# FFN input products: shared sums carried between PSUM banks, seven products in another order

## Chip, core and metric

The kernel runs as one program on one core of a Trainium2 chip. The metric is the time of one execution in device microseconds (us). TensorE multiplies, VectorE and ScalarE do the elementwise work, GpSimd does next to nothing here, and SyncE issues the DMAs. In the rows PE is TensorE, PEld its weight loads, DVE VectorE, ACT ScalarE, POOL GpSimd, and SPq the DMA queue of SyncE.

## What is computed

One Conformer-style layer over 1056 tokens (1024 of a prompt and 32 of a running stream): a half-step SwiGLU feed-forward block (FFN 1), a mixer of a convolution branch and a recurrent branch, a second feed-forward block (FFN 2), and norms between them. The change lies in the first half of both feed-forward blocks:

```python
D_MODEL = 1024
D_FF = 2816
...
def _swiglu_half_step(x, g_pre, g_post, w_in, w_out):
    h = _rmsnorm(x, g_pre)
    gate, up = jnp.split(h @ w_in, 2, axis=-1)
    return x + 0.5 * _rmsnorm((jax.nn.silu(gate) * up) @ w_out, g_post)
```

## The kernel before

Channels lie on the 128 lanes and tokens along the rows, in four quarters of 264 tokens. All products keep float32's accuracy: each operand is split into a high and a low part, and each term of a product takes three matmuls (`mm3`, L202 wh·xh, L203 wh·xl, L204 wl·xh), each 128x128 by 128x264. Splitting an operand is one copy on ScalarE (L91, the high part) and one subtraction on VectorE (L88, the low part).

An FFN's hidden layer has 22 chunks of 128 channels. The first few (three in FFN 1, two in FFN 2) are plain products. For each of the others, 39 in all, `w_ops` makes seven weight operands w1 to w7 from the gate and up columns of the chunk (Winograd's form of a 2 by 2 cut: rows gate and up, inner halves of the channels, columns two quarters of the tokens). The operands w1, w2 and w4 are split straight from the weights as loaded. The other four come from sums on VectorE in one buffer `s` and one `s3`: w5 from s = a21 + a22, w6 from s - a11 (in place, after w5's parts are read), w7 from s3 = a11 - a21, w3 from a12 - s (in place again). Then `swiglu` runs twice, for the two pairs of quarters (call 0 and call 1 below), 78 calls in all. A call runs seven products of 12 matmuls each, and combines them to silu(gate) * up for two quarters (`prod`), which a DMA stores in DRAM (`hd`, L437). Names in the rows: `p` is a product's PSUM bank, `w` and `xh`/`xl` are operands, `m`, `g`, `u` are sums of products. In the listings of instructions `p6_1_10_0` is product 6 of FFN 1, chunk 10, call 0.

The PSUM pool `ps` has six banks (L63). In each call before, every product gets its own bank: order 1, 2, 4, 5, 6, 7, 3. ScalarE copies product 1 out to `m`, and VectorE forms all sums from `m` and the banks, in nine instructions.

Each engine runs its instructions in the order of its queue, and waits on semaphores. What stands ahead of what in a queue is set by priorities at build time: weight operands are made ready some 100 to 350 instructions early (`WLATE`, `WAHEAD`, `AHEAD`), and everything else comes in the order of the code.

After the hidden chunks the output half of the FFN (bank `po`, operands `hh`, `hl` from loads `hf`, and `wh_o`, `wl_o` from loads `w_o`) multiplies by w_out. SyncE issues the stores `hd`, and the loads `hf` and `w_o`, from one queue.

Of the kernel before, what the change touches and what calls it, by code (L numbers as in the profile page):

```python
# [11 lines left out]
OP = mybir.AluOpType  # L12
# [22 lines left out]
# how many instructions early operands are made ready: weights, those of the seven products, the hidden, w_out's  # L35
AHEAD, WAHEAD, WLATE, HAHEAD, OAHEAD = 350, 120, 100, 100, 150
# terms of products that TensorE runs while a norm's squares, its power, a chain of two norms, a mean, a layer norm
# are on the way, and between the norms of two quarters
SQ, TURN, CHAIN, MUW, LNW, STAG = 12, 6, 30, 16, 32, 32
# chunks of the output that the last two quarters take one after the other; chunks side by side at a pass's start  # L40
TAIL1, TAIL2, TAILW, OG = 4, 3, 2, 2
# hidden chunks by plain products at the start of either FFN
NP = (3, 2)
# taps of the long convolution between the steps of the mixer
# [8 lines left out]
def macaron_kernel(ctx: ExitStack, tc: tile.TileContext, a: dict, o: dict):  # L53
# [43 lines left out]
    def over(x, n):  # L97
        """A [P, w] row seen n times."""
        return bass.AP(tensor=x.tensor, offset=x.offset, ap=[list(x.ap[0]), [0, n], list(x.ap[1])])
# [75 lines left out]
    def load(dst, src):  # L175
        """A load that does not run ahead of the weights traced before it."""
        with tc.issue_after(newest[0]):
            nc.sync.dma_start(dst, src)
# [11 lines left out]
    def after(n, f):  # L190
        """f(), traced when TensorE has n more terms of products to run."""
        later.append((terms[0] + n, f))
# [8 lines left out]
    def mm3(out, wh, wl, xh, xl, first, last):  # L201
        nc.tensor.matmul(out, wh, xh, start=first, stop=False)  # L202
        nc.tensor.matmul(out, wh, xl, start=False, stop=False)  # L203
        newest_mm[:] = [nc.tensor.matmul(out, wl, xh, start=False, stop=last).ins]  # L204
        terms[0] += 1
        for e in [e for e in later if e[0] <= terms[0]]:
            later.remove(e)
            e[1]()
# [33 lines left out]
    def rstd(ssum, name, then, wait=SQ):  # L242
        """then(1 / rms on every lane); TensorE runs other products while the squares are summed and the power is taken."""
# [26 lines left out]
    def pre_norm(x, g, name, then, wait=SQ):  # L270
        """then(half, x / rms * g as a float32 quad), for either half of the channels."""
# [17 lines left out]
    def pre_norm_parts(x, g, name, rb, stored=False):  # L289
        """Parts of x * rb * g; x: quads, or the slice of them that DRAM holds."""  # L290
# [16 lines left out]
    def evacuate(y, c, p, gain, sq, q, name, total=None):  # L307
        """One chunk of the channels of a quarter, times its gain, to y; its squares to the quarter's sum."""
# [11 lines left out]
    def post_norm(y, q, ssum, xsrc, xdst, name, then):  # L320
        """y <- x + y / rms, for one quarter of the tokens, y times its gain already; then()."""
# [16 lines left out]
    #   rows: gate | up; inner: halves of the channels; columns: two quarters of the tokens  # L338
# [8 lines left out]
    def x_part(r, v, half, odd, name):  # L347
        """The parts of half a quarter: two operands each, but for an odd quarter's first half, which only plain products take."""
# [5 lines left out]
    def x_sums(r, fe, fo, name):  # L354
# [12 lines left out]
        tt(t, t, fe[1], OP.subtract)  # L367
# [31 lines left out]
    def swiglu(w, x, prod, name):  # L399
        """prod <- silu(gate) * up of one hidden chunk, two quarters of the tokens."""  # L400
        b = {}

        def product(k):
            b[k] = BANK(f"p{k}_{name}")[:, :N]
            for j in range(HC):
                s = slice(j * P, (j + 1) * P)
                mm3(b[k], w[k][:, 0, s], w[k][:, 1, s], x[k][0][:, j, :], x[k][1][:, j, :], j == 0, j == HC - 1)

        m, g0, g1, u1 = (TMP(f"{n}_{name}") for n in ("m", "g0", "g1", "u1"))
        product("1")  # L410
        copy(m, b["1"])
        product("2")
        tt(g0, m, b["2"], OP.add)
        nc.scalar.activation(g0, g0, AF.Silu)
        product("4")
        product("5")
        product("6")
        tt(m, m, b["6"], OP.add)
        tt(g1, m, b["5"], OP.add)
        product("7")  # L420
        tt(m, m, b["7"], OP.add)
        tt(u1, m, b["5"], OP.add)
        tt(m, m, b["4"], OP.subtract)
        tt(prod[:, 0, :], g0, m, OP.mult)
        product("3")
        tt(g1, g1, b["3"], OP.add)
        nc.scalar.activation(g1, g1, AF.Silu)  # L427
        return tt(prod[:, 1, :], g1, u1, OP.mult).ins

# [1 line left out]
    def ffn(x, f, h, first, mid, w_in, w_out, early, between, finish, tail, n):  # L431
# [41 lines left out]
        for c in range(2):  # L473
# [16 lines left out]
            def out(tiles, blks, which, c=c, hid=hid, y=y):  # L490
                """Tiles (m, q) of the output, together where the hidden chunks are still coming in."""
# [81 lines left out]
    def pieces(q, gap):  # L573
        """The columns of quarter q in a row that keeps `gap` past columns between the two streams."""
# [17 lines left out]
    # the 31 taps by pairs of columns: with E, O the taps at even and odd distances,  # L592
    #   even = E u_even + O u_odd (one pair back), odd = (E + O)(u_even + u_odd) - E u_even - O u_odd
# [346 lines left out]
```

## Time and profile before

| | |
|---|---|
| runs | 2369.85 and 2373.73 us, median 2371.79 us |
| span of the profiled execution | 2369.3 us, first to last instruction; no other time of it is given, and the runs' median lies 2.5 us above it |
| TensorE busy | 2329.1 us (98%) in 19136 matmuls |
| VectorE busy | 1607.6 us (68%) |
| ScalarE busy | 932.3 us (39%) |
| chain that ended last | TensorE 95% |

Matmuls overlap: one is recorded with 0.28 us, while the next starts 0.12 us after it. So a stage is costed by the spacing of the starts, and the busy share shows only where TensorE stood still.

### The profile page before, as it was taken

To read this page: it belongs to the slowest core of one execution; us is meant where nothing else is said; L and a number is where in the kernel's file an instruction comes from. 1 tells how busy PE (TensorE), PEld (TensorE's weight loads), DVE (VectorE), ACT (ScalarE), POOL (GpSimd) and SP (SyncE) were. 2 spreads that over 40 slices of the span, in tenths; PEclk is the share of its full clock that TensorE was granted. 3 is DMA by queue.
4 is the path that set the end of the run, shared out by engine and by line. 5 is a ranking of instruction groups with operands and counts; after the bars stand their busy time and mean duration, and the time that the engine had idled before them with its cause. 6 is when DMAs were issued, how large, how long until landed. Compare 5 with 4: busy or idle time off the path is not lost.

```text
span 2369.3 us, 45071 instructions
## 1 busy us (share of the span) xinstructions
PE 2329.1 (98%) x19136; PEld 2322.5 (98%) x19136; DVE 1607.6 (68%) x2652; ACT 932.3 (39%) x1536; POOL 42.3 (2%) x63
## 2 busy tenths in 40 slices
PE   7999999999999999999999999999999999999996
PEld 7999999999999999999999999999999999999996
DVE  6776666752647887897778966458866666752646
ACT  4333333342444554345544343244333333342432
POOL 0000000000000000000000000001000000000000
PEclk9999999999999999999999999999999999999998
DMA  5122222363655222222222554444122222363453
GB/s 173 60 73 77 82 82 82 106 205 100 230 170 177 74 91 70 85 73 82 75 72 77 179 201 164 146 129 145 59 80 82 82 82 82 96 206 109 168 174 128
DMA packets 126089, 274.13 MB, mean 116 GB/s; under 512 B 16704, under 2 KB 58432, under 8 KB 125888
## 3 DMA queue, kind: packets, MB, share of 16 engines
q1 hardware_dynamic: 125888, 271.26, 35.0%
q8 instruction: 149, 2.44, 0.4%
q14 instruction: 52, 0.43, 0.1%
HBM read 212.55 MB, written 58.67 MB: 114 GB/s over the span
## 4 chain that ended last, share of the span: by engine, by line
PE 95%; DVE 2%; DMA 1%; issue 1%; ACT 0%; POOL 0%; SPq 0%; POOLq 0%; DVEq 0%; ACTq 0%
PE p L202 11%; PE p L204 11%; PE p L203 11%; PE po L203 7%; PE po L202 7%; PE po L204 7%; PE pm L202 3%; PE pm L204 3%; PE pm L203 3%; PE pco L202 1%; PE pco L204 1%; PE pcv L202 1%; PE pcg L202 1%; PE pro L202 1%; PE pco L203 1%; PE prx L202 1%
## 5 line engine op out<-in xcount | busy, mean ns | idle before, releaser
L202 PE MATMUL p<-xh,w 128*128 128x264 f32 x2184 | 620.9, 284 | 1.1 <-ACT w L91 0.8
L203 PE MATMUL p<-xl,w 128*128 128x264 f32 x2184 | 618.7, 283 | 0.1
L204 PE MATMUL p<-xh,w 128*128 128x264 f32 x2184 | 618.5, 283 | 0.0
L202 PEld LDWEIGHTS p<-xh,w 128*128 128x128 f32 x2184 | 410.1, 188 | 2.4 <-ACT w L91 2.4
L203 PEld LDWEIGHTS p<-xl,w 128*128 128x128 f32 x2184 | 411.1, 188 | 0.3 <-DVE xl L88 0.3
L204 PEld LDWEIGHTS p<-xh,w 128*128 128x128 f32 x2184 | 410.0, 188 | 0.0
L203 PE MATMUL po<-hl,wh_o 128*128 128x264 f32 x1408 | 399.4, 286 | 1.8 <-DVE hl L88 1.8
L204 PE MATMUL po<-hh,wl_o 128*128 128x264 f32 x1408 | 398.2, 285 | 0.0
L202 PE MATMUL po<-hh,wh_o 128*128 128x264 f32 x1408 | 393.1, 287 | 1.9 <-ACT hh L91 1.9
L203 PEld LDWEIGHTS po<-hl,wh_o 128*128 128x128 f32 x1408 | 266.2, 189 | 2.6 <-DVE hl L88 2.5
L204 PEld LDWEIGHTS po<-hh,wl_o 128*128 128x128 f32 x1408 | 266.1, 189 | 0.0
L202 PEld LDWEIGHTS po<-hh,wh_o 128*128 128x128 f32 x1408 | 262.1, 189 | 2.7 <-ACT hh L91 2.5
L88 DVE TENSOR_TENSOR wl_o<-w_o,wh_o 128x1024 fp32r<-128x1024 f32 x109 | 132.9, 1224 | 115.3 <-ACT wh_o L91 115.0
L88 DVE TENSOR_TENSOR m<-m,p 128x264 f32<-128x264 f32 x234 | 99.8, 426 | 162.7 <-PE p L204 161.0
L612 DVE SCALAR_TENSOR_TENSOR pq<-u,vec,pq 128x542 f32<-128x542 f32 (+14 forms) x232 | 172.1, 777 | 0.0
L427 ACT ACTIVATE g<-g 128x264 f32<-128x264 f32 x78 | 33.2, 426 | 347.6 <-DVE g L88 347.5
L91 ACT ACTIVATE wh_o<-w_o 128x1024 fp32r<-128x1024 f32 x109 | 115.3, 1064 | 124.0 <-PE po L203 108.1
L88 DVE TENSOR_TENSOR w<-s,w 128x512 fp32r<-128x512 f32 x156 | 104.2, 689 | 49.3 <-ACT w L91 49.3
L91 ACT ACTIVATE w<-s 128x512 fp32r<-128x512 f32 x156 | 94.3, 628 | 80.2 <-DVE s L88 77.5
L88 DVE TENSOR_TENSOR s<-s,s 128x264 f32<-128x264 f32 x56 | 24.0, 431 | 101.2 <-ACT s L313 101.1
L612 DVE SCALAR_TENSOR_TENSOR rs<-rs,wsum 128x542 f32<-128x542 f32 (+6 forms) x112 | 87.0, 777 | 0.0
L88 DVE TENSOR_TENSOR g<-m,p 128x264 f32<-128x264 f32 x156 | 66.7, 428 | 21.5 <-PE p L204 18.1
(448 smaller groups left out, 5729.3 us busy)
## 6 DMA issues: line engine op xcount, KB each, us to landing
w_o<-in_w_ffn_out SPq DMA_DIRECT2D x109, 512.0 KB, 3.6
hf<-hd SPq DMA_DIRECT2D x44, 528.0 KB, 5.3
hd<-prod SPq DMA_DIRECT2D x78, 264.0 KB, 3.9
w_g<-in_w_ffn_in SPq DMA_DIRECT2D x39, 512.0 KB, 3.5
w_u<-in_w_ffn_in SPq DMA_DIRECT2D x39, 512.0 KB, 4.1
w_wo<-in_w_out SPq DMA_DIRECT2D x18, 512.0 KB, 3.5
sgd<-sg SPq DMA_DIRECT2D x32, 264.0 KB, 2.3
gs<-sgd SPq DMA_DIRECT2D x16, 528.0 KB, 6.9
```

The source lines that it names most:

```text
L88: return nc.vector.tensor_tensor(out, x, y, op=op)
L91: return nc.scalar.activation(out, x, AF.Copy)
L202: nc.tensor.matmul(out, wh, xh, start=first, stop=False)
L203: nc.tensor.matmul(out, wh, xl, start=False, stop=False)
L204: newest_mm[:] = [nc.tensor.matmul(out, wl, xh, start=False, stop=last).ins]
L427: nc.scalar.activation(g1, g1, AF.Silu)
L612: nc.vector.scalar_tensor_tensor(acc[c][:, d:], src[c][:, :HW - d], wt[c](d), acc[c][:, d:], op0=OP.mult, op1=OP.add)
```

## The change

One call has four banks instead of seven, and runs its products in the order 1, 5, 6, 2, 7, 3, 4. Product 1 is summed in bank p1, and ScalarE copies p1 into bank p6 (PSUM to PSUM). TensorE adds product 6 onto that, ScalarE copies the sum into bank p7, and VectorE adds s5 (product 5, copied out by ScalarE) to p6 in place. TensorE then adds product 2 onto p1, product 7 onto p7, product 3 onto p6 and product 4 onto p7. SiLU reads the banks directly. VectorE keeps four instructions of nine, and ScalarE has five instead of three. The sign of x operand 4 is turned, since TensorE can add only. TensorE's instructions keep their number.

```diff
-        nc.tensor.matmul(out, wh, xh, start=first, stop=False)
-        nc.tensor.matmul(out, wh, xl, start=False, stop=False)
-        newest_mm[:] = [nc.tensor.matmul(out, wl, xh, start=False, stop=last).ins]
+        nc.tensor.matmul(out, wh, xh, start=first, stop=False, skip_group_check=True)
+        nc.tensor.matmul(out, wh, xl, start=False, stop=False, skip_group_check=True)
+        newest_mm[:] = [nc.tensor.matmul(out, wl, xh, start=False, stop=last, skip_group_check=True).ins]
...
-        tt(t, t, fe[1], OP.subtract)
+        tt(t, fe[1], t, OP.subtract)
...
-                mm3(b[k], w[k][:, 0, s], w[k][:, 1, s], x[k][0][:, j, :], x[k][1][:, j, :], j == 0, j == HC - 1)
-
-        m, g0, g1, u1 = (TMP(f"{n}_{name}") for n in ("m", "g0", "g1", "u1"))
-        product("1")
-        copy(m, b["1"])
-        product("2")
-        tt(g0, m, b["2"], OP.add)
-        nc.scalar.activation(g0, g0, AF.Silu)
-        product("4")
-        product("5")
-        product("6")
-        tt(m, m, b["6"], OP.add)
-        tt(g1, m, b["5"], OP.add)
-        product("7")
-        tt(m, m, b["7"], OP.add)
-        tt(u1, m, b["5"], OP.add)
-        tt(m, m, b["4"], OP.subtract)
-        tt(prod[:, 0, :], g0, m, OP.mult)
-        product("3")
-        tt(g1, g1, b["3"], OP.add)
-        nc.scalar.activation(g1, g1, AF.Silu)
-        return tt(prod[:, 1, :], g1, u1, OP.mult).ins
...
+                mm3(b, w[k][:, 0, s], w[k][:, 1, s], x[k][0][:, j, :], x[k][1][:, j, :], first and j == 0, j == HC - 1)
+
+        s5, g0, g1, u1 = (TMP(f"{n}_{name}") for n in ("s5", "g0", "g1", "u1"))
+        p1, p5 = bank("1"), bank("5")
+        product("1", p1, True)
+        p6 = bank("6")
+        copy(p6, p1)
+        product("5", p5, True)
+        copy(s5, p5)
+        product("6", p6, False)
+        p7 = bank("7")
+        copy(p7, p6)
+        tt(p6, p6, s5, OP.add)
+        product("2", p1, False)
+        nc.scalar.activation(g0, p1, AF.Silu)
+        product("7", p7, False)
+        tt(u1, p7, s5, OP.add)
+        product("3", p6, False)
+        nc.scalar.activation(g1, p6, AF.Silu)
+        product("4", p7, False)
+        tt(prod[:, 1, :], g1, u1, OP.mult)
+        return tt(prod[:, 0, :], g0, p7, OP.mult).ins
```

Priorities place the instructions anew. ScalarE's queue from the last SiLU of chunk 9 into chunk 10 of FFN 1 stood so before:

```order
L427 ACTIVATE g1_1_9_1_2705<-g1_1_9_1_2705 128x264 [waits DVE_49]
L91 ACTIVATE w5_1_10_2826<-s_1_10_2824 128x512 [waits DVE_49]
L91 ACTIVATE m_1_10_0_2843<-p1_1_10_0_2847 128x264 [waits PE_49]
L414 ACTIVATE g0_1_10_0_2844<-g0_1_10_0_2844 128x264 [waits DVE_49]
L91 ACTIVATE w6_1_10_2830<-s_1_10_2824 128x512 [waits DVE_49]
L91 ACTIVATE w7_1_10_2836<-s3_1_10_2833 128x512
L91 ACTIVATE w3_1_10_2839<-s_1_10_2824 128x512 [waits DVE_49]
```

ScalarE's queue at the same place in the changed kernel:

```order
L428 ACTIVATE g1_1_9_1_2627<-p6_1_9_1_2643 128x264 [waits DVE_49,PE_49]
L91 ACTIVATE w5_1_10_2742<-s_1_10_2740 128x512 [waits DVE_49]
L91 ACTIVATE p6_1_10_0_2777<-p1_1_10_0_2763 128x264 [waits PE_49]
L91 ACTIVATE w6_1_10_2746<-s_1_10_2740 128x512 [waits DVE_49]
L91 ACTIVATE w7_1_10_2752<-s3_1_10_2749 128x512
L91 ACTIVATE s5_1_10_0_2759<-p5_1_10_0_2764 128x264 [waits PE_49,Activation_49]
L91 ACTIVATE w3_1_10_2755<-s_1_10_2740 128x512 [waits DVE_49]
L91 ACTIVATE p7_1_10_0_2804<-p6_1_10_0_2777 128x264 [waits PE_49,Activation_49]
```

The weight operands kept their order, and the three copies between banks stand among them. 35 of the 39 chunks read so; the first and the last of each FFN also have the activations' splits or the output weights in between.

TensorE's queue from the end of product 5 of the same call, before (product 5 is the fourth of the call there):

```order
L203 MATMUL p5_1_10_0_2889<-xl5_1_0_818,w5_1_10_2826 128x264
L204 MATMUL p5_1_10_0_2889<-xh5_1_0_817,w5_1_10_2826 128x264
L202 MATMUL p6_1_10_0_2902<-xh6_1_0_822,w6_1_10_2830 128x264 [waits Activation_49]
L203 MATMUL p6_1_10_0_2902<-xl6_1_0_823,w6_1_10_2830 128x264
L204 MATMUL p6_1_10_0_2902<-xh6_1_0_822,w6_1_10_2830 128x264 [waits DVE_49]
L202 MATMUL p6_1_10_0_2902<-xh6_1_0_822,w6_1_10_2830 128x264
```

TensorE's queue there now (product 5 is the second of the call):

```order
L204 MATMUL p5_1_10_0_2764<-xh5_1_0_817,w5_1_10_2742 128x264
L202 MATMUL p6_1_10_0_2777<-xh6_1_0_822,w6_1_10_2746 128x264 [waits Activation_49]
L203 MATMUL p6_1_10_0_2777<-xl6_1_0_823,w6_1_10_2746 128x264
L202 MATMUL p1_1_10_0_2763<-xh2_1_0_163,w2_1_10_2734 128x264
L203 MATMUL p1_1_10_0_2763<-xl2_1_0_164,w2_1_10_2734 128x264
L204 MATMUL p1_1_10_0_2763<-xh2_1_0_163,w2_1_10_2734 128x264
L204 MATMUL p6_1_10_0_2777<-xh6_1_0_822,w6_1_10_2746 128x264 [waits DVE_49]
```

Three matmuls of product 2 were moved ahead of product 6's third matmul, which waits for the low part of w6.

SyncE's queue from the store of the last hidden chunk of FFN 1, before:

```order
L437 DMA hd1_116<-prod1_21_1_5690 128x528 [waits DVE_49]
L478 DMA hf1_0_5_5829<-hd1_116 128x2x528 [waits PE_49]
L478 DMA hf1_0_6_5835<-hd1_116 128x2x528 [waits DMAHW1_49,PE_49]
L172 DMA w_o1_0_9_6370<-in_w_ffn1_out 128x1024 [waits DMAHW3_49,DMAHW2_49,DVE_49]
L478 DMA hf1_0_7_5841<-hd1_116 128x2x528 [waits PE_49]
```

SyncE's queue there now:

```order
L440 DMA hd1_116<-prod1_21_1_5468 128x528 [waits DVE_49]
L172 DMA w_o1_0_8_6036<-in_w_ffn1_out 128x1024 [waits DMAHW7_49,DMAHW1_49,DVE_49]
L481 DMA hf1_0_5_5601<-hd1_116 128x2x528 [waits DMAHW0_49,PE_49]
L481 DMA hf1_0_6_5607<-hd1_116 128x2x528 [waits PE_49]
L481 DMA hf1_0_7_5613<-hd1_116 128x2x528 [waits DMAHW2_49,PE_49]
L172 DMA w_o1_0_9_6142<-in_w_ffn1_out 128x1024 [waits DMAHW3_49,DVE_49]
```

The load hf 7 now stands ahead of w_o 9, and w_o 8 has moved behind the store.

## Rows read from the trace of the kernel before

**Rows 1.** Page, part 1: busy us, share of the span, instructions

```profile
span 2369.3 us, 45071 instructions
PE 2329.1 (98%) x19136; PEld 2322.5 (98%) x19136; DVE 1607.6 (68%) x2652; ACT 932.3 (39%) x1536; POOL 42.3 (2%) x63
```

**Rows 2.** Waits of PE: waiting <- releaser, us in total, times, longest

```profile
PE po L202 <- ACT hh L91: 1.9, 2, 1.1
PE po L203 <- DVE hl L88: 1.8, 2, 0.9
...
PE p L202 <- ACT w L91: 0.8, 2, 0.5
```

**Rows 3.** Windows: length, busy us of PE, PEld, DVE, ACT, POOL, clock, DMA

```profile
120.00:460.00 340.00, 340.00 (x2810) 340.00 (x2809) 232.68 (x534) 105.08 (x215) 1.67 (x1) 1.00 0.25 78
455.00:475.00 20.00, 19.39 (x155) 18.74 (x154) 17.68 (x29) 10.58 (x15) 0.00 (x0) 1.00 0.53 171
500.00:520.00 20.00, 18.02 (x134) 17.60 (x134) 7.39 (x6) 7.50 (x10) 0.10 (x1) 0.91 0.47 168
510.00:600.00 90.00, 90.00 (x741) 90.00 (x740) 26.79 (x30) 28.84 (x46) 0.00 (x0) 1.00 0.39 126
2084.00:2110.00 26.00, 24.27 (x185) 23.85 (x184) 12.27 (x14) 9.32 (x9) 0.40 (x4) 0.93 0.58 197
```

**Rows 4.** Timeline, PE, from one chunk of FFN 1 to the next: start, us

```profile
315.23 0.28 PE L204 MATMUL p<-xh,w 128*128 128x264 f32 x1
315.35 0.28 PE L202 MATMUL p<-xh,w 128*128 128x264 f32 x1
```

**Rows 5.** Timeline, DVE, the same place

```profile
315.55 0.43 DVE L88 TENSOR_TENSOR g<-g,p 128x264 f32<-128x264 f32 x1
315.90 0.43 DVE L88 TENSOR_TENSOR prod<-g,m 128x264 f32<-128x264 f32 x1
...
317.79 0.68 DVE L88 TENSOR_TENSOR w<-s,w 128x512 fp32r<-128x512 f32 x1
...
318.88 0.68 DVE L88 TENSOR_TENSOR s<-s,w_g 128x512 f32<-128x512 f32 x1
320.26 1.29 DVE L88 TENSOR_TENSOR w<-s,w 128x512 fp32r<-128x512 f32 x2 [0.70 <-ACT w L91]
321.47 0.69 DVE L88 TENSOR_TENSOR s<-w_g,s 128x512 f32<-128x512 f32 x1
```

**Rows 6.** Timeline, ACT, the same place

```profile
316.01 0.43 ACT L427 ACTIVATE g<-g 128x264 f32<-128x264 f32 x1 [6.77 <-DVE g L88]
316.96 0.63 ACT L91 ACTIVATE w<-s 128x512 fp32r<-128x512 f32 x1 [0.52 <-DVE s L88]
317.50 0.37 ACT L91 ACTIVATE m<-p 128x264 f32<-128x264 f32 x1
...
319.59 1.15 ACT L91 ACTIVATE w<-s 128x512 fp32r<-128x512 f32 x2 [0.17 <-DVE s L88]
```

**Rows 7.** Timeline, last chunk of FFN 1, where PE waited for a weight operand

```profile
463.27 1.15 ACT L91 ACTIVATE w<-s 128x512 fp32r<-128x512 f32 x2 [0.18 <-DVE s L88]
...
463.95 0.39 PE L202 MATMUL p<-xh,w 128*128 128x264 f32 x1
464.18 0.28 PE L203 MATMUL p<-xl,w 128*128 128x264 f32 x1
```

**Rows 8.** Timeline, DVE, first seven-product chunk of FFN 1

```profile
97.16 1.25 DVE L88 TENSOR_TENSOR t<-t,f_a 128x1056 f32<-128x1056 f32 x1
```

**Rows 9.** Timeline, DVE, last chunk of FFN 1

```profile
460.43 1.26 DVE L88 TENSOR_TENSOR hl<-hf,hh 128x1056 fp32r<-128x1056 f32 x1
```

**Rows 10.** Timeline, PE and SyncE, end of FFN 1's hidden half

```profile
479.63 0.29 PE L202 MATMUL po<-hh,wh_o 128*128 128x264 f32 x1
...
484.28 0.33 SPq L437 DMA_DIRECT2D hd<-prod  x1
...
494.26 1.48 SPq L478 DMA_DIRECT2D hf<-hd  x1
```

More of the change, by code (lines that the diff above doesn't have):

```diff
@@ L399, in swiglu, with bank, product @@
     def swiglu(w, x, prod, name):
-        b = {}
-        def product(k):
-            b[k] = BANK(f"p{k}_{name}")[:, :N]
+        def bank(k):
+            return BANK(f"p{k}_{name}")[:, :N]
+        def product(k, b, first):
             for j in range(HC):
                 s = slice(j * P, (j + 1) * P)
-                mm3(b[k], w[k][:, 0, s], w[k][:, 1, s], x[k][0][:, j, :], x[k][1][:, j, :], j == 0, j == HC - 1)
-        m, g0, g1, u1 = (TMP(f"{n}_{name}") for n in ("m", "g0", "g1", "u1"))
-        product("1")
-        copy(m, b["1"])
-        product("2")
-        tt(g0, m, b["2"], OP.add)
-        nc.scalar.activation(g0, g0, AF.Silu)
-        product("4")
-        product("5")
-        product("6")
-        tt(m, m, b["6"], OP.add)
-        tt(g1, m, b["5"], OP.add)
-        product("7")
-        tt(m, m, b["7"], OP.add)
-        tt(u1, m, b["5"], OP.add)
-        tt(m, m, b["4"], OP.subtract)
-        tt(prod[:, 0, :], g0, m, OP.mult)
-        product("3")
-        tt(g1, g1, b["3"], OP.add)
-        nc.scalar.activation(g1, g1, AF.Silu)
-        return tt(prod[:, 1, :], g1, u1, OP.mult).ins
+                mm3(b, w[k][:, 0, s], w[k][:, 1, s], x[k][0][:, j, :], x[k][1][:, j, :], first and j == 0, j == HC - 1)
[19 more added lines that the diff above has]
+        return tt(prod[:, 0, :], g0, p7, OP.mult).ins
     def ffn(x, f, h, first, mid, w_in, w_out, early, between, finish, tail, n):
```

## Prediction

> **What bounds the kernel now.** The page's first part comes first [rows 1]: TensorE is busy 2329.1 of 2369.3 us, VectorE 68%, ScalarE 39%. TensorE is the bound, and the 40 us that it idles are mostly the first input's way in and the last norms. The question is whether TensorE waits for anything in the stage that changes. The waits of TensorE answer it [rows 2]: matmuls into `p` waited 0.8 us in the whole run, once in the last chunk of each FFN. The windows show the same [rows 3]: from 120 to 460 us it is busy 340.00 of 340.00 us, at full clock (1.00, the level of 2.4 GHz). 2810 matmuls in 340 us are 0.121 us each, so a product of 12 takes 1.45 us and a chunk of two calls 20.3 us. In the output half, with VectorE busy 27 of 90 us instead of 233 of 340, they take 90/741 = 0.1215 us. So the spacing doesn't hang on VectorE's load, and a VectorE with less to do gives nothing back by itself.
>
> **What is removed and added off the path.** VectorE loses 5 of 9 instructions a call, at 0.43 us [rows 5]: 78 x 5 x 0.43 = 168 us. ScalarE gains two copies a call, at the 0.37 us of its copy out of PSUM [rows 6]: 58 us. Neither engine is the bound in this stage (68% and 31% of the window before), so both sums count zero. TensorE's matmuls keep their number. The turned sign, the checks switched off and the fewer banks cost nothing: the same instructions run, and six banks still hold a call and a half.
>
> At this point the Trainium skill, in "TensorE: Matmul & The Clock Gate", section "Back-to-back issue gap", gives N/2.4 + 2.5 ns for a warm matmul, so 112.5 ns for 264 columns by that page, where this trace has 121. If VectorE's traffic were what makes up that difference, lightening it could free up to 8.5 ns on each of 6552 matmuls; the output half's 121.5 ns under a light VectorE speaks against it.
>
> **What moves onto the path: w5 and w6 are needed earlier.** Product 5 was fourth in a call and is now second; product 6 was fifth and is third. The operands w5 and w6 of a chunk are made as late as before, behind the last SiLU of the chunk ahead (both listings of ScalarE's queue). I follow one change of chunk, with t = 0 at the first matmul of product 4 of the call ahead, which is now the last. That is the moment product 3 has been issued.
> - A reader of a finished product starts 0.20 us after the next product's first matmul (315.35 to 315.55) [rows 4, 5]. SiLU 0.43 us [rows 6], hand-over 0.04: at 0.67 VectorE starts a product of `prod`.
> - From there to w5's low part VectorE has the same four instructions as before, 315.90 to 317.79 = 1.89 us [rows 5]. So w5 low runs from 2.56 to 3.24 us.
> - TensorE wants it after products 4 and 1 and two matmuls, at 3.14 us: 0.15 us late with hand-over.
> - The sum for w6 (in place, after w5 is read) starts at 3.27; from it to w6's low part took 318.88 to 320.26 = 1.38 us [rows 5], with the high part on ScalarE between [rows 6]. So w6 low runs from 4.65 to 5.33, and is there at 5.38 us.
> - TensorE wants it after three products (4.35), two matmuls of product 6 and the three of product 2 that were moved ahead: 4.95 us. It is late by 0.43 us.
> - A matmul that waited for a weight costs more: 463.95 to 464.18 is 0.23 us to the next, instead of 0.12 [rows 7]. With 0.11: 0.54 us a chunk.
>
> What hides the three new copies: p1 to p6 is done at 2.90 + 0.20 + 0.37 = 3.47, and ScalarE waits for w6's sum until 3.98 anyway. p6 to p7 stands behind w3's copy: sum for w3 at 4.65 + 1.21 = 5.86 [rows 5], w3's copy from 6.58, the bank's copy 0.54 later (316.96 to 317.50) [rows 6], done at 7.50; product 7 is due at 5 x 1.45 + 0.54 = 7.79, a cover of 0.24 us. The addition in place on p6 is done near 8.3, product 3 is due at 9.25. No row shows a copy from PSUM to PSUM or an addition into PSUM; 0.37 and 0.43 us are the nearest, and up to 0.24 us more is covered. In the second call no weights are in the way: each copy has a product of 1.45 us as cover and needs 0.20 + 0.37.
>
> So 35 regular chunks cost 35 x 0.54 = **+18.9 us**. The bounds of one chunk: 0.3 us if hand-overs are a little quicker, since three of them add up here; 0.93 us if one weight copy of 0.63 us more stands ahead of the copy to p7 (0.54 + 0.63 - 0.24). I take 0.54, since each link has its own row.
>
> **The edges.** In the first seven-product chunk of FFN 1 the addition on p6 stands behind VectorE's last `t` (97.16 + 1.25 us [rows 8]) and is ready at 99.4, with product 3 due at 98.8: +0.8 with restart. In FFN 2's first I find 0.3 us of cover. In each FFN's last chunk one `hl` of 1.26 us [rows 9] stands between w6's sum and its low part, and copies of output weights, which wait for DMA, stand between the bank copies: about 2.9 us of waiting against 0.7 before, **+4.4** for two; I give it 1 to 5 us each.
>
> **What comes back.** Before, the last `prod` came late: its store left at 484.28, 4.65 us after the first output matmul, and blocked the loads `hf` behind it; the one at 494.26 [rows 10] left TensorE waiting for `hh` and `hl`, 1.98 us in the window 500 to 520, with the granted clock down to 0.91 there, (1 - 0.91) x 20 = 1.8 us more [rows 2, 3]. FFN 2 has the same at 2084 to 2110: 1.73 and (1 - 0.93) x 26 = 1.8 us. Now VectorE has fewer sums at the end, the store can leave within about 1 us, and hf 7 no longer stands behind w_o 9. At most 7.3 us come back, at least 0 if w_o 8, which has moved ahead, holds the queue. I take three quarters: **-5.5**.
>
> **Sum.** 18.9 + 0.8 + 4.4 - 5.5 = +18.6 us on the profiled 2369.3: 2388. The runs' median lies 2.5 us above the span, so 2390 us, 0.8% slower. A difference of 2% is 47 us; that is about what a measurement tells from no change.
>
> **Rivals.**
> - The waits are hidden anyway: priorities and queues give w6 some 0.4 us sooner than my chain, the edges give back 7 us, and the time is 2365 to 2376. For it: the moved matmuls of product 2 already cover 0.36 us. Against: the chain's pieces are all measured.
> - A longer chain: the copy to p7 behind w3 is late too, 0.93 us a chunk, 33 us, and the last chunks cost 5 us each: 2402 to 2415. It decides where the bank copy and its hand-overs need 0.24 us more than the copy out of PSUM.
> - Slower by more than 2%: each pause lets the clock fall. The row for it is 500 to 520: waits of 1.1 and 0.9 us, then a clock of 0.91, 1.8 us lost. At 35 chunks that is 63 us on top of 18.6: 2453. Against it the window 455 to 475: 0.61 us of pauses, and the clock stays 1.00. So it decides between pauses of 0.5 and 1.1 us in one place, and mine are 0.15 to 0.5.
> - The lighter VectorE speeds up the matmuls. The bound is the spacing of the shortest row, and rows of both stages give 0.121, so nothing; 2390 stands. By the page's 112.5 ns it would be 6552 x 8.5 ns = 56 us less, near 2334, and the trace disagrees with that.
> - The change doesn't do what it says, and VectorE keeps its work: excluded by its queue, which has 390 rows fewer, 5 x 78.
>
> **How the numbers follow.** My forecast (2376 to 2402) 66%, hidden 13%, longer chain 13%, over 2% slower (clock, or waits in both calls) 7%, faster matmuls 1%. The range reaches from 2373 into the hidden case to 2411 in the longer one, and leaves out about 19%. Faster by over 2% 0.01, within 2% 0.92, slower by over 2% 0.07.
>
> **What would show it.** The waits of TensorE should list `p` waiting for w at L204 and L202, 15 to 25 us in some 70 to 110 times, in call 0 alone; the distance of two chunks should read 20.8 us instead of 20.3; the granted clock should stay 1.00 there. The waits for `hh` and `hl` should shrink. The forecast is wrong if the waits name a bank copy as releaser in both calls, if the clock in 120 to 460 falls below 1.00, or if TensorE stays busy without a gap.

## The result and the profile after

The changed kernel takes 2394.47 us (median of 2 runs, 2392.75 to 2396.18) against 2371.79 before: ratio 1.0093, interval 1.0065 to 1.0121. It is 0.9% slower, where 2390 us and 0.8% had been forecast. The interval lies wholly above 1, so the change is told from none, although the prediction put that limit at about 2%. The profiled execution took 2396.18 us, its span 2394.4.

The page of the changed kernel, part 1, and two groups of its part 5 (line, engine, operation, count | busy us, mean ns | idle us before, and what ended most of it):

```profile
span 2394.4 us, 44896 instructions
PE 2350.4 (98%) x19136; PEld 2332.3 (97%) x19136; DVE 1468.3 (61%) x2262; ACT 980.3 (41%) x1692; POOL 42.3 (2%) x63
...
L202 PEld LDWEIGHTS p<-xh,w 128*128 128x128 f32 x2184 | 413.1, 189 | 11.2 <-ACT p L91 6.9
L204 PEld LDWEIGHTS p<-xh,w 128*128 128x128 f32 x2184 | 411.8, 189 | 7.3 <-DVE w L88 1.5
```

VectorE has 139 us less to do, ScalarE 48 us more, TensorE as many matmuls as before [rows 1]. TensorE is shown busy for 21 us longer, and the idle time in front of the loads of `p`'s weights (18.5 us in these two lines) is almost all new.

The waits of TensorE in the changed kernel (us in total, times, longest):

```profile
PE p L202 <- ACT p L91: 5.3, 4, 2.7
...
PE po L202 <- ACT hh L91: 0.8, 1, 0.8
...
PE po L203 <- DVE hl L88: 0.5, 2, 0.3
```

Against [rows 2]: the waits for `hh` and `hl` have gone from 3.7 to 1.3 us, four waits on a copy between banks are new, and no wait for a `w` is listed at all. The windows tell why that is not the whole story (length, busy us and instructions of each engine, granted clock, DMA):

```profile
223.00:239.00 16.00, 16.00 (x135) 16.00 (x134) 6.11 (x13) 5.21 (x13) 0.00 (x0) 1.00 0.16 51
307.00:323.00 16.00, 16.00 (x132) 16.00 (x132) 5.84 (x13) 5.20 (x12) 0.00 (x0) 1.00 0.15 53
120.00:460.00 340.00, 340.00 (x2722) 335.13 (x2721) 168.95 (x357) 123.24 (x275) 1.67 (x1) 1.00 0.25 77
...
500.00:520.00 20.00, 19.83 (x164) 19.62 (x163) 7.73 (x7) 7.97 (x8) 0.29 (x3) 1.00 0.56 193
2084.00:2130.00 46.00, 43.93 (x352) 42.97 (x351) 27.93 (x34) 21.66 (x30) 0.39 (x4) 1.00 0.68 224
```

From 120 to 460 us TensorE reads busy 340.00 of 340.00 us, as before [rows 3], but it ran 2722 matmuls there and not 2810: 88 x 0.121 = 10.6 us lost in a row that shows no idle time. A matmul's bar (0.28 us) is longer than the distance to the next (0.121), so pauses of less than about 0.15 us leave no hole between the bars. The count gives them away, and so do the bars of the weight loads (335.13 busy instead of 340.00). The clock reads 1.00 in all these rows.

The pauses themselves, in the timeline of TensorE at one change of chunk (start us, length us):

```profile
303.56 0.28 PE L203 MATMUL p<-xl,w 128*128 128x264 f32 x1
303.75 0.39 PE L204 MATMUL p<-xh,w 128*128 128x264 f32 x1
303.98 0.29 PE L202 MATMUL p<-xh,w 128*128 128x264 f32 x1
...
304.95 0.29 PE L204 MATMUL p<-xh,w 128*128 128x264 f32 x1
305.14 0.39 PE L202 MATMUL p<-xh,w 128*128 128x264 f32 x1
305.37 0.28 PE L203 MATMUL p<-xl,w 128*128 128x264 f32 x1
...
305.73 0.53 PE L204 MATMUL p<-xh,w 128*128 128x264 f32 x2
306.09 0.28 PE L202 MATMUL p<-xh,w 128*128 128x264 f32 x1
```

and in those of VectorE and ScalarE at the same place:

```profile
301.12 0.43 DVE L88 TENSOR_TENSOR prod<-g,u 128x264 f32<-128x264 f32 x1 [1.46 <-ACT g L428]
...
303.01 0.69 DVE L88 TENSOR_TENSOR w<-s,w 128x512 fp32r<-128x512 f32 x1
303.73 0.69 DVE L88 TENSOR_TENSOR s<-s,w_g 128x512 f32<-128x512 f32 x1
...
305.12 1.29 DVE L88 TENSOR_TENSOR w<-s,w 128x512 fp32r<-128x512 f32 x2 [0.70 <-ACT w L91]
```

```profile
300.69 0.39 ACT L428 ACTIVATE g<-p 128x264 f32<-128x264 f32 x1 [2.56 <-PE p L204]
302.19 0.63 ACT L91 ACTIVATE w<-s 128x512 fp32r<-128x512 f32 x1 [1.10 <-DVE s L88]
303.64 0.38 ACT L91 ACTIVATE p<-p 128x264 f32<-128x264 f32 x1 [0.82 <-PE p L204]
```

The third matmul of product 5 (303.75) starts when w5's low part is done (303.01 + 0.69), the first of product 6 (305.14) behind w6's high part (on ScalarE from 304.46), the next L204 of product 6 behind w6's low part (305.12 + 0.69 = 305.81). Each time the distance to the matmul that follows is 0.22 to 0.23 instead of 0.12.

In the regular chunks a count over the starts of all matmuls of the stretch (distances over 0.145 us taken as pauses, less 0.1211 each) gives 0.45 us of pauses a chunk in both FFNs. The distances between pauses are counted in the windows 120 to 460 and 1720 to 2050 us, which hold 30 whole stretches. It gives a second loss: between pauses the mean distance is 121.1 ns in 5 of 30 chunks and 122.6 to 122.9 ns in the other 25. The two windows of 16 us above lie between pauses, in a chunk of either kind: 135 and 132 matmuls. Chunks follow at 20.82 to 20.83 us where it is 121.1, and at 20.95 to 21.12 us otherwise.

Where the 25.0 us between the two spans lie. The hidden half with seven products runs from the first matmul of `p` to the first of `po`: in FFN 1 from 91.54 to 479.63 before, from 91.94 to 495.22 after (+15.2 us); in FFN 2 from 1672.43 to 2081.47 before, from 1685.36 to 2108.64 after (+14.2 us). By the same count these 29.4 us are pauses in the regular chunks 16.0, slower distances 8.2, the last chunks 8.25 instead of 2.85 (+5.4), the first chunks -0.2. The stretches behind them, from a first `po` to the next FFN or the end, took 4.8 us less. The stage ahead of the first `p` took 0.4 us more.

### The profile page after: what moved, and what is told of

It is laid out like the page before. It is cut to its first block, busy times and chain, and to the rows that moved or that the text cites. A ratio compares the mean times of both kernels' runs of the same rounds, so it can differ in the third digit from the quotient of the medians.

```text
span 2394.4 us, 44896 instructions
## 1 busy us (share of the span) xinstructions
PE 2350.4 (98%) x19136; PEld 2332.3 (97%) x19136; DVE 1468.3 (61%) x2262; ACT 980.3 (41%) x1692; POOL 42.3 (2%) x63
## 4 chain that ended last, share of the span: by engine, by line
PE 94%; DMA 2%; DVE 2%; issue 1%; ACT 1%; POOL 0%; SPq 0%; POOLq 0%; DVEq 0%; ACTq 0%
PE p L204 11%; PE p L202 11%; PE p L203 11%; PE po L203 7%; PE po L202 7%; PE po L204 7%; PE pm L202 3%; PE pm L204 3%; PE pm L203 3%; PE pcv L202 1%; PE pro L202 1%; PE pcg L202 1%; PE prx L202 1%; PE prg L202 1%; PE pcv L204 1%; PE pcg L204 1%
## 5 line engine op out<-in xcount | busy, mean ns | idle before, releaser
L202 PE MATMUL p<-xh,w 128*128 128x264 f32 x2184 | 627.8, 288 | 5.6 <-ACT p L91 5.3
L204 PE MATMUL p<-xh,w 128*128 128x264 f32 x2184 | 627.1, 289 | 0.1
L204 PEld LDWEIGHTS p<-xh,w 128*128 128x128 f32 x2184 | 411.8, 189 | 7.3 <-DVE w L88 1.5
L204 PE MATMUL po<-hh,wl_o 128*128 128x264 f32 x1408 | 397.1, 284 | 0.0
L204 PEld LDWEIGHTS po<-hh,wl_o 128*128 128x128 f32 x1408 | 264.9, 188 | 0.0
L88 DVE TENSOR_TENSOR p<-p,s 128x264 f32<-128x264 f32 x78 | 34.1, 438 | 159.6 <-ACT p L91 159.6
L91 ACT ACTIVATE p<-p 128x264 f32<-128x264 f32 x156 | 58.4, 375 | 168.2 <-PE p L204 168.1
L428 ACT ACTIVATE g<-p 128x264 f32<-128x264 f32 x78 | 30.4, 390 | 147.5 <-PE p L204 147.5
```

Of the source, the lines that this page charges most:

```text
L88: return nc.vector.tensor_tensor(out, x, y, op=op)
L91: return nc.scalar.activation(out, x, AF.Copy)
L202: nc.tensor.matmul(out, wh, xh, start=first, stop=False, skip_group_check=True)
L428: nc.scalar.activation(g1, p6, AF.Silu)
```

## Experiments

Two questions are told apart. Do the pauses come from the order of the products (w5 and w6 needed sooner than made) or from the copies between banks? And does the slower distance belong to the new order and its additions onto banks, or to the pauses? Each kernel's table row at the end of this section counts pauses and distances as above. All are edits of the changed kernel, unless said otherwise.

**Order alone.** The old evacuation in the new order (shortened: lines are joined, removed lines left out):

```diff
+        own("1"); copy(g0, b["1"])
+        own("5"); own("6")
+        tt(m, g0, b["6"], OP.add); tt(g1, m, b["5"], OP.add)
+        own("2"); tt(g0, g0, b["2"], OP.add); nc.scalar.activation(g0, g0, AF.Silu)
+        own("7"); tt(m, m, b["7"], OP.add); tt(u1, m, b["5"], OP.add)
+        own("3"); tt(g1, g1, b["3"], OP.add); nc.scalar.activation(g1, g1, AF.Silu)
+        own("4"); tt(m, m, b["4"], OP.add)
```

> The new order of products (1, 5, 6, 2, 7, 3, 4) with the old evacuation: a bank for each product, nine sums and products on VectorE a call, no copy between banks. Theory (order is the cost): pauses at every change of chunk, longer than with the copies, because VectorE has an addition before the last SiLU (0.45 us) and one between the sums of the weights (0.35 us): 0.45 + 0.8 = about 1.2 us a chunk, 2405 to 2425 us. Rival (copies are the cost): no pauses, 2372. If spacing comes with the pauses, it should read 122.8 ns in some chunks here too, without any copy between banks; if it comes from the copies, 121.1.

Measured: 2413.24 us, ratio 1.0165 (1.0142 to 1.0189), as the theory had it. The waits and two matmuls of TensorE:

```profile
PE p L204 <- DVE w L88: 13.8, 37, 0.4
```

```profile
308.97 0.28 PE L203 MATMUL p<-xl,w 128*128 128x264 f32 x1
309.62 0.39 PE L204 MATMUL p<-xh,w 128*128 128x264 f32 x1 [0.37 <-DVE w L88]
```

With no copy between banks in the program, TensorE waits at the same places for the same operands, 1.1 us a chunk. This wait is long enough to be listed. The distance is 122.5 to 122.8 ns in 26 of 30 chunks.

**No copies between banks.** Products 6 and 7 start their banks afresh, so their sums leave out product 1, and products 1 and 6; only the time is of use.

```diff
-        copy(p6, p1)
...
-        product("6", p6, False)
+        product("6", p6, True)
...
-        copy(p7, p6)
...
-        product("7", p7, False)
+        product("7", p7, True)
```

> The changed kernel without its two copies from bank to bank: products 6 and 7 start their banks afresh (their sums lack product 1 and products 1 and 6). Theory (copies are off the path in regular chunks): the pauses stay, 0.4 to 0.5 us a chunk, and only the waits on bank copies in the last chunk of each FFN, 2.9 and 1.3 us, go: 2388 to 2392. Rival (spacing of 122.8 ns comes from the copies): 121.1 ns, 8 us less, 2380 to 2384. Rival (copies hold TensorE in every chunk): 2370 to 2375.

Measured: 2380.92 us, ratio 1.0028 (1.0016 to 1.0041), 7 us under the theory's range. The number lies in the range of the rival that put the slower distance down to the copies, but not for its reason, as the distance shows. Pauses stay, 0.34 us a chunk. The 0.11 us by which they are shorter is about one matmul: with the dependency gone, four instead of three matmuls of product 2 stand ahead of w6's low part in TensorE's order. The slower distance stays, in 25 of 30 chunks, so the copies between banks don't make it. The last chunks have 0.6 us of pauses left of 8.25: there the copies cost more than the 4.2 us that had been put down to them.

**Sums early.** The tile `prod` is taken when it is first written, and the next chunk's `s` gets its buffer after it, so `s` could not be made before the product of `g1` and `u1`. Here `u1` is written into `prod`:

```diff
-        tt(u1, p7, s5, OP.add)
+        tt(prod[:, 1, :], p7, s5, OP.add)
...
-        tt(prod[:, 1, :], g1, u1, OP.mult)
+        tt(prod[:, 1, :], g1, prod[:, 1, :], OP.mult)
```

> The changed kernel with u1 written straight into the second half of prod, so that the tile prod is taken earlier and the sum s of the next chunk, which takes its buffer behind it, can be made before the last SiLU; w5's copy then stands ahead of g1 on ScalarE. Theory (the pauses at a change of chunk are w5 and w6 made too late; the order of the products is what costs): the three pauses of 0.45 us together go from 35 chunks, 16 us; if the slower spacing of matmuls, 122.8 instead of 121.1 ns, comes with the pauses, another 8 us goes: about 2370 us. Rival 1 (the slower spacing comes from copies and additions in PSUM banks): pauses gone, spacing stays 122.8 ns: about 2378. Rival 2 (the copies between banks hold TensorE): pauses stay, 2394.

Measured: 2366.38 us over 10 runs, ratio 0.9972 (0.9959 to 0.9985): 0.3% under the kernel before and 28 us under the changed one. VectorE at a change of chunk, and three windows:

```profile
314.45 0.43 DVE L88 TENSOR_TENSOR prod<-p,s 128x264 f32<-128x264 f32 x1 [2.00 <-PE p L204]
314.80 0.68 DVE L88 TENSOR_TENSOR s<-w_u 128x512 f32<-128x512 f32 x1
...
316.18 0.69 DVE L88 TENSOR_TENSOR w<-s,w 128x512 fp32r<-128x512 f32 x1
316.79 0.42 DVE L88 TENSOR_TENSOR prod<-g,prod 128x264 f32<-128x264 f32 x1
```

```profile
120.00:460.00 340.00, 339.14 (x2796) 338.72 (x2795) 171.16 (x360) 121.03 (x279) 1.67 (x1) 1.00 0.23 77
...
475.00:500.00 25.00, 24.66 (x190) 24.66 (x191) 13.63 (x14) 11.95 (x16) 0.40 (x4) 0.93 0.60 205
...
1720.00:2050.00 330.00, 330.00 (x2727) 330.00 (x2727) 163.56 (x306) 118.89 (x274) 0.00 (x0) 1.00 0.23 79
```

The sum now follows the addition on p7 and no longer a SiLU. In FFN 2 not one pause is left in the regular chunks, and the distance is 121.1 ns in all of them, with the same order and the same copies. That decides the first question: the lateness of w5 and w6, and nothing about the copies, made the regular pauses. In FFN 1 one chunk still loses 1.4 us, where small constants are made on VectorE. Ahead of that pause, and behind one of 0.22 us in the first chunk, 330 matmuls ran at 122.7 ns (99.3 to 139.8 us); behind it all read 121.1. By the count the last chunks still lose 6.4 us. In FFN 1 there is one pause of 2.07 us, and behind it 14 matmuls 0.22 us apart, the level of 1.2 GHz (the 0.93 of the row from 475); these 14 are in the 6.4.

**Copies in another order.** To keep the copies and need w6 later: 1, 2, 5, 6, 4, 7, 3, with product 4 in a bank of its own (lines joined as above).

```diff
+        product("1", p1, True);  copy(p6, p1)
+        product("2", p1, False); nc.scalar.activation(g0, p1, AF.Silu)
+        product("5", p5, True);  copy(s5, p5)
+        product("6", p6, False); copy(p7, p6); tt(p6, p6, s5, OP.add)
+        product("4", p4, True);  copy(s4, p4)
+        product("7", p7, False); tt(s5, p7, s5, OP.add); tt(s4, p7, s4, OP.add)
+        product("3", p6, False); nc.scalar.activation(g1, p6, AF.Silu)
```

> Copies between banks kept, order 1, 2, 5, 6, 4, 7, 3: w6 is needed one product (1.45 us) later than in the changed kernel, product 4 has a bank of its own, as cover for the copy to p7, and is added by VectorE. Theory (order): no pauses at the change of regular chunks, spacing 121.1 ns, the gain at the change to the output half kept: 2360 to 2374. Rival (copies): pauses stay, 2390 or more.

Measured: 2400.97 us, ratio 1.0109 (1.0086 to 1.0132). The forecast missed. The waits, then TensorE and ScalarE where product 2 begins:

```profile
PE p L202 <- ACT p L91: 10.9, 38, 0.6
```

```profile
305.88 0.28 PE L203 MATMUL p<-xl,w 128*128 128x264 f32 x1
306.44 0.39 PE L202 MATMUL p<-xh,w 128*128 128x264 f32 x1 [0.28 <-ACT p L91]
```

```profile
304.92 0.64 ACT L91 ACTIVATE w<-s 128x512 fp32r<-128x512 f32 x1
306.01 0.38 ACT L91 ACTIVATE p<-p 128x264 f32<-128x264 f32 x1 [0.46 <-PE p L204]
```

Product 2 adds onto p1, which must have been copied first. With product 2 straight behind product 1 the copy (0.20 + 0.38) has only two matmuls as cover, in both calls of a chunk, and a pause of 0.45 us in the one and 0.2 us in the other remains, each with a restart of 0.1. The waits for weights are gone, as the theory says. The distance is about 122.5 ns behind each first pause and 121.2 behind each second, chunk after chunk. I had taken away the cover that the changed kernel's order gives: product 5 between 1 and 2 is there for the copy.

**That order mended.** 1, 5, 2, 6, 4, 7, 3, and product 2 kept behind product 5:

```diff
...
+        product("5", p5, True); copy(s5, p5)
+        with behind():
+            product("2", p1, False)
...
```

> The kernel of the run before with copies in another order, mended: 1, 5, 2, 6, 4, 7, 3, so that the copy of p1 has product 5 as cover again, while w6 is needed one product later than in the changed kernel and w5 at the same place. Theory (two operands, each with its own lateness): the pause for w5 stays, 0.17 us a chunk, the two for w6 go, 0.28 us: 35 x 0.28 = 10 us less than the changed kernel, 2384, with 122.7 ns after the pause that is left; 2376 if a short pause lets the spacing be 121.1. Rival (the copy of p1 stands behind w5's on ScalarE and is what TensorE waits for): 0.3 us or more a call, 2395 or more.

Measured: 2388.74 us, ratio 1.0060 (1.0040 to 1.0080). Only one place is left where TensorE waits, w5's low part:

```profile
303.50 0.28 PE L203 MATMUL p<-xl,w 128*128 128x264 f32 x1
304.11 0.39 PE L204 MATMUL p<-xh,w 128*128 128x264 f32 x1 [0.33 <-DVE w L88]
```

The pauses for w6 have gone, but w5's is 0.58 us and not 0.17. The expectation overlooked that `s` comes behind the first writing of `prod`, and that here two additions and a product stand ahead of it on VectorE: it starts 1.36 us after the first matmul of the last product (300.47 to 301.83), where the changed kernel needs 0.98 (300.49 to 301.47). Those 0.4 us are what the pause grew by. The copies are not what it waits for, so the rival falls.

**Late sums in the kernel before.** The other way round: make w5 and w6 late in the old order, with the old evacuation.

```diff
             s = mid("s")
-            tt(s, a21, a22, OP.add)
+            for _ in range(6):
+                tt(s, a21, a22, OP.add)
```

> The kernel before, with the first sum of the weights (s, from which w5 and w6 are made) computed six times instead of once: five more VectorE instructions of 0.6 us a chunk, so that w5 and w6 are made 3.0 us later, which is about the two products (2.9 us) by which the changed kernel needs them sooner. Order of products and evacuation are those of before, no copy between banks. Theory (late operands alone make the pauses, and the spacing of 122.7 ns follows a pause): pauses of 0.3 to 1.0 us a chunk and 122.7 ns in most chunks: 2385 to 2415. Rival 1 (the slower spacing belongs to the new order or to additions onto a bank): pauses, but 121.1 ns: 2380 to 2405. Rival 2 (there is more slack than worked out): no pauses, 2372.

Measured: 2515.53 us, ratio 1.0593 (1.0571 to 1.0615): the pauses come, but 3.6 us a chunk. VectorE shows the mistake in the amount:

```profile
308.59 0.68 DVE L88 TENSOR_TENSOR s<-w_u 128x512 f32<-128x512 f32 x1
...
310.40 0.42 DVE L88 TENSOR_TENSOR prod<-g,u 128x264 f32<-128x264 f32 x1
310.74 0.69 DVE L88 TENSOR_TENSOR s<-w_u 128x512 f32<-128x512 f32 x1
311.35 0.42 DVE L88 TENSOR_TENSOR g<-m,p 128x264 f32<-128x264 f32 x1
311.69 2.14 DVE L88 TENSOR_TENSOR s<-w_u 128x512 f32<-128x512 f32 x3
```

A sum, a product and an addition that used to follow `s` now stand between its repetitions, so it ends 4.55 us later and not 3.0 (313.83 instead of 309.28). The slack of w5 was 2.1 us: TensorE would have wanted it at 312.06, and its high part would have been ready at 309.95. The rest, 2.45, is the first pause.

With three sums instead of six, worked out from those rows:

> The kernel before with the first sum of the weights made three times instead of once. From the run with six: w5's high part had 2.1 us of slack (needed at 312.06, ready at 309.95 without the extra sums), and s came 4.55 us later, since a sum, a product and an addition that used to follow came in between. With three it comes about 2.1 us later: w5's high part just in time, its low part 0.5 us late, w6 0.2 to 0.5 us late, three restarts of 0.1: 0.8 to 1.3 us a chunk. Theory (the spacing is set at a restart, whatever the order and the evacuation): in some chunks 122.7 ns here too, in the old order and without copies: 2400 to 2425. Rival (122.7 ns belongs to the order 1, 5, 6, 2, 7, 3, 4 or to additions onto a bank): 121.1 ns in all chunks, 2400 to 2415.

Measured: 2413.87 us (2 runs), ratio 1.0179 (1.0150 to 1.0209), pauses of 1.1 to 1.2 us a chunk: the amount follows the lateness once the queue is read in full. The distances, in these two runs of the old order, are 121.0 to 121.4 ns nearly everywhere, but 122.6 to 122.8 in 2 of 28 and 2 of 30 stretches. So the slower distance occurs without the new order, but seldom.

The kernel before has it too, outside the regular chunks. A window of the mixer, where both run the same matmuls in the same order, first in the kernel before, then in the one with the sums early:

```profile
1440.00:1570.00 130.00, 130.00 (x1061) 130.00 (x1060) 59.76 (x101) 39.31 (x60) 0.00 (x0) 1.00 0.37 126
```

```profile
1440.00:1570.00 130.00, 130.00 (x1076) 130.00 (x1075) 59.96 (x103) 41.13 (x63) 0.00 (x0) 1.00 0.38 130
```

By the count over starts the kernel before ran 1123 matmuls in a row at 122.8 ns there (1436.2 to 1574.1 us) without a pause, and again up to the first pause in FFN 2's first seven-product chunk (1645.7 to 1685.7); behind that pause it ran at 121.1. With the sums early the mixer's stretch ran at 121.1. This answers the second question: the slower distance needs neither the new order nor additions onto banks, and the same code runs at either distance.

**Small steps in the changed kernel.** To change the pauses and neither the products' order nor the copies, eight columns of `s` are multiplied by 1.0: once behind the first sum, once or twice behind the second.

```diff
+            nc.vector.tensor_scalar(s[:, :8], s[:, :8], 1.0, None, op0=OP.mult)
```

> The changed kernel with one small instruction more in the chain of w5: eight columns of s are multiplied by 1.0 in place (0.16 us, values unchanged). The sum s3, 0.6 us, then goes between s and it. Theory (pauses are the lateness of the operands, one for one): w5 and all behind it 0.7 us later, the pauses grow by 0.5 to 0.7 us a chunk: 2411 to 2420. On the spacing: if it is set at the restart by how long the pauses were, fewer or other chunks at 122.7 ns than the 25 of 30 of the changed kernel; if it belongs to the order of the products and the copies, about 25 of 30 again.

> The same small instruction, but in the chain of w6 alone, behind the second sum. Theory: w6 0.2 us later with the hand-over; five instead of three matmuls of product 2 are moved ahead of w6's low part and cover 0.24 us of it: pauses of 0.4 to 0.55 us a chunk, 2392 to 2398. Spacing: as in the run before, if set at the restart, a share of chunks at 122.7 ns that differs from 25 of 30 in at least one of the three runs; if it belongs to order and copies, about 25 of 30.

> Two such instructions in the chain of w6. Theory: w6 0.3 to 0.4 us later, six matmuls of product 2 moved ahead: pauses of 0.45 to 0.65 us a chunk, 2394 to 2402. Spacing as in the two runs before.

Measured, one run each beside 2373.54 us for the kernel before: 2394.68, 2387.88 and 2394.13 us. The first two lie below their forecasts (2411 to 2420 and 2392 to 2398), the third at the lower end of its own. The middle one has longer pauses than the changed kernel (0.57 us a chunk instead of 0.45) and was 8 us shorter in its profiled span (2386.1 against 2394.4). Its window over FFN 2, where the changed kernel ran 2634 matmuls:

```profile
1720.00:2050.00 330.00, 330.00 (x2648) 324.10 (x2647) 164.86 (x319) 119.13 (x269) 0.00 (x0) 1.00 0.25 78
```

By the count over all starts it loses 4.1 us more to regular pauses, 5.9 us less to the slower distance (8 of 30 chunks at 122.2 ns and more instead of 25), and 4.6 us less in the last chunks. The order and the copies are the same, a small step moves the pauses, and the distance is another in most chunks. Within each trace it is set where TensorE restarts, and holds to the next pause. That the step itself made the difference between the two traces is likely and not shown: each kernel was traced once, and whether another execution of it would show the same share was not tried. In the first of the three, less came of the step than forecast: w5's chain was longer by s3 and the step, but more matmuls of product 2 had been put ahead, and the pauses grew by 0.3 us.

**The edge.** The copies `hh` of the last chunk, from the third on, behind the last copy between banks, in the kernel with the sums early:

```diff
-        copy(p7, p6)
+        bank_copy[:] = [copy(p7, p6).ins]
...
+                with tc.issue_after(bank_copy[0]) if c == 0 and g >= 2 else nullcontext(), tc.high_priority(offset=HAHEAD):
                     split(hi, lo, w)
```

> The kernel of the first experiment (sums early), and in each FFN's last chunk the copies hh of the hidden, from the third on, are queued behind the last copy from bank to bank. Theory (what is left at the edge is a bank copy behind an hh that waits for its DMA on ScalarE's queue, 1.95 and 1.28 us of pause, and 1.6 us of clock at 1.2 GHz behind the first of them): 4 to 5 us less than the first experiment, 2361 to 2363, 0.4% under the kernel before. Rival (the hidden operands are then late for the output half, which waits as long as the hidden half did): as the first experiment, 2366.

Measured: 2364.99 us, ratio 0.9960 (0.9944 to 0.9976); the two intervals overlap, so the 1.4 us to the first version are not told from nothing. What the last chunks lose by the count went from 6.4 to 1.4 us, and the clock stayed at 1.00 there. The waits say where the gain went:

```profile
PE po L203 <- DVE hl L88: 1.7, 2, 0.9
...
PE po L202 <- ACT hh L91: 1.1, 2, 0.8
```

In the two traces the gain is given back behind the edge, as the rival said (the spans are 2364.5 and 2365.5 us): the hidden operands are late for the output half.

| kernel | us | pauses in a regular chunk, us | stretches between pauses at 122.1 to 122.9 ns |
|---|---|---|---|
| before | 2371.8 | 0 | none |
| changed | 2394.5 | 0.45 | 25 of 30 |
| order alone | 2413.2 | 1.10 | 26 of 30 |
| no copies between banks | 2380.9 | 0.34 | 25 of 30 |
| sums early | 2366.4 | 0 (one chunk: 1.4) | none but the one that ends at 139.8 us |
| order 1, 2, 5, 6, 4, 7, 3 | 2401.0 | 0.87 | 30 of 58 |
| order 1, 5, 2, 6, 4, 7, 3 | 2388.7 | 0.58 | 9 of 30 |
| before, six sums | 2515.5 | 3.6 | 2 of 28 |
| before, three sums | 2413.9 | 1.2 | 2 of 30 |
| step for w5 | 2394.7 | 0.76 | 18 of 30 |
| step for w6 | 2387.9 | 0.57 | 8 of 30 |
| two steps for w6 | 2394.1 | 0.66 | 8 of 30 |

## Why the prediction was right, and where it was not

The forecast (2390, between 2373 and 2411, slower by 0.8%) holds, and its main mechanism is shown. Between the spans the change is 25.0 us where the sum had 18.6. A missing term of 8.2 us, the slower distance, is in part hidden by pauses that came out 2.9 us smaller. That the total is only some 5 us off is partly luck.

- **The chain to w5 and w6** was right in its times. With product 4's first matmul as zero (300.69 less 0.20 for the SiLU = 300.49): w5's low part was due from 2.56 and ran from 2.52 (303.01), the sum for w6 from 3.27 and ran from 3.24, w6's low part from 4.65 and ran from 4.63. The kernel with the sums early shows that it sets the pauses.
- **35 x 0.54 = 18.9 us** measured 16.0: 0.45 us a chunk. The lateness was right. It breaks into three pauses, but the last ends when w6's low part is there, however many came before it; and part of the lateness (41 matmuls at 1.6 ns, 0.07 us) stands in the slower distance and not in a pause. Behind a chunk at 121.1 ns the pauses are 0.48 to 0.50 us instead of 0.45, as that asks.
- **The distance of 0.121 us "everywhere"** was the step that failed. The argument from the two stages of before, that it doesn't hang on VectorE's load, holds. But it was taken as a constant from two windows, while the mixer of the same trace ran at 122.8 ns (1061 matmuls in 130 us), and no row of before shows a stretch that follows short pauses chunk after chunk. The term that this left out is +8.2 us, a third of the change.
- **Off the path**, VectorE was to lose 168 us and ScalarE to gain 58; 139 and 48 were measured. The sums used the length of a bar, 0.43 us, but instructions that follow each other start 0.35 us apart (315.55 and 315.90 in [rows 5]): 390 x 0.35 = 136. ScalarE's SiLU reads a bank now and took 0.39 us (300.69) instead of 0.43 [rows 6], which the sum left out: 156 x 0.04 = 6 us less. Neither sum was on the path, as said.
- **The cover of the copies** held in regular chunks: the copy between banks took 0.375 us (0.37 taken) and the addition in place 0.438 (0.43 taken), and no wait on them is listed outside the last chunks. That their cover depends on product 5 between 1 and 2 was not in the text; with it taken away the pauses were 0.87 us a chunk.
- **The last chunks**, +4.4 forecast, +5.4 measured (3.4 and 2.0), but for a reason that was only half named. The 0.7 us before was read from busy time, which hides short pauses: by the count they lost 1.48 and 1.37 us before, and 4.93 and 3.32 after, where 2.9 each had been forecast. ScalarE and TensorE in the second call of FFN 1's last chunk:

```profile
488.12 1.08 ACT L91 ACTIVATE hh<-hf 128x1056 fp32r<-128x1056 f32 x1 [4.04 <-DMA hf<-hd]
...
490.32 0.38 ACT L91 ACTIVATE p<-p 128x264 f32<-128x264 f32 x1
```

```profile
487.74 0.28 PE L204 MATMUL p<-xh,w 128*128 128x264 f32 x1
490.75 0.39 PE L202 MATMUL p<-xh,w 128*128 128x264 f32 x1 [2.73 <-ACT p L91]
```

ScalarE stood for 4.04 us before an `hh` whose load had not landed, with the copies of the banks behind it. The prediction had copies of output weights there. The main cause is the hidden's load, and moving `hh` behind the copies, in the kernel with the sums early, took 5 us of loss away at this place.
- **The first chunks**: +0.8 forecast in FFN 1 and nothing in FFN 2; +0.2 and -0.4.
- **What comes back**: -5.5 forecast, -4.8 measured behind the hidden halves. The last store left 0.74 us after the first output matmul (forecast: within about 1), the next loads of the hidden 1.7 us later:

```profile
495.96 0.32 SPq L440 DMA_DIRECT2D hd<-prod  x1
...
497.69 1.44 SPq L481 DMA_DIRECT2D hf<-hd  x3
```

 and the clock reads 1.00 where it was 0.91 and 0.93 [rows 3]. That the earlier store is the cause was read from the traces and not tried by itself.
- **What would show it** named the wrong view: the list of waits was to hold 15 to 25 us of `p` waiting for w, and holds none, and "TensorE busy without a gap" was to refute the forecast, which it seemed to do. Pauses of 0.07 us each don't open a gap between bars. The distance of two chunks was the right sign: 20.8 us in five chunks, 20.95 to 21.12 in the others.
- **Rivals**: the waits were not hidden; the copy to p7 was in time; the clock stayed at 1.00 at these pauses, and also at one of 3.01 us, so the bound of 0.5 to 1.1 us that the prediction drew for it does not hold; a lighter VectorE freed nothing.

What stays open: what puts TensorE in the slower distance. Of the 25.0 us, 8.2 have no cause shown. The kernel before with late sums had it seldom, the changed kernel mostly, the one with a step of 0.16 us on VectorE in 8 chunks of 30, the mixer in one of the two traces shown. No rule was found, and whether it differs between executions of one kernel was not tried.

## What to carry to other kernels

Moving a product forward moves its operands' due time forward: walk the queues that make the operand before the order is changed, and where it comes too late, look for what holds the first instruction of its chain. Here that was a buffer handed out in program order, and writing one sum into a tile that exists anyway turned 0.9% slower into 0.3% faster than before. A copy that lets later products add onto a bank needs cover between its source's end and the next write of either bank: here it took 0.20 + 0.38 us, for which two matmuls were too little and one product was enough. And in a queue executed in order an instruction that waits for a DMA should not stand ahead of it, though here moving that one only moved the wait. Where a profile's bars overlap, count instructions in a window, since busy time can't show such losses.

## What the hardware showed unexpectedly

- The distance of matmuls of 264 columns, each with its own weights, has several steady values at a granted clock of 1.00: after a restart 120.6, 121.1, 121.6, 122.2 or about 122.7 ns, held to the next pause. In the order 1, 5, 2, 6, 4, 7, 3 chunks of FFN 1 alternate from 303 us on: 122.8 ns behind a distance of 0.61 us, 121.1 behind one of 0.58. Long streams without pauses were seen at two of them: 121.1 ns in the regular chunks before, 122.8 ns in the mixer of the same trace.
- In the Trainium skill, "TensorE: Matmul & The Clock Gate", section "Back-to-back issue gap", N/2.4 + 2.5 ns is the gap of an isolated warm matmul, which gives an estimate of 112.5 ns for 264 columns. For a stream of weight loads and matmuls the same section of the Trainium skill has about 81 ns at 128 columns and 131 ns at 512. The prediction used the first for a stream; a straight line between the other two would give an estimate of 99 ns. No steady stretch of the hidden halves comes near either: the shortest distances are 120.5 to 121.1 ns, with VectorE busy 68% of a stretch of the stage (before) or 50% (changed).
- Whether a pause lets the clock fall is not told by its length alone: after the pause of 3.01 us in the changed kernel (487.74 to 490.75) the granted clock stays 1.00 and the matmuls 0.12 us apart, after one of 2.07 us at the same edge with the sums early 14 of them come at 0.22 us (1.2 GHz).
- A restart after a wait for a weight costs 0.10 us beyond the wait: the next distance is 0.22 to 0.23 us.
- ScalarE copied 128x264 from bank to bank in 0.375 us and from a bank to SBUF in 0.382 us (medians of the stretch from 120 to 460 us): no difference worth planning for.
